# Stated VectorE order and chunk-innermost scan states in an S5/gMLP encoder layer

## The chip, the cores and the metric

The kernel runs on one core of a Trainium2 chip. The metric is the device time of one execution in microseconds (us). The engines are TensorE (PE in the profile; PEld is its weight load), VectorE (DVE), ScalarE (ACT), GpSimd (POOL) and SyncE (SP, which only issues DMAs).

## The reference, cut to what matters

One encoder layer over 512 tokens of width 1024, in float32. The change touches the S5 branch and whatever shares VectorE with it.

```python
n = rms_norm(h, mix_norm_g[i])
proj = n @ w_in[i]                      # xa | zu | zv | gate_a | gate_b
ya = s5_branch(xa, ...)                 # two directions of a diagonal recurrence, 32 groups of 16 channels, 64 states each
yb = sgu_branch(zu, zv, ...)            # gelu, layer norm, 128x128 position mixing per head
merged = gate_a * (ya @ w_proj_a[i]) + gate_b * (yb @ w_proj_b[i])
h = h + merged @ w_out[i]
h = h + memory_cross_attention(...)
h = h + swiglu(...)
return rms_norm(h, final_norm_g)
```

In the S5 branch a state follows `s[t] = lam_bar * s[t-1] + b_bar u[t]` in complex numbers, forward for the first direction and backward for the second, and the output is `Re(c s) + d u`.

## The kernel before, in words

**Weights.** Each float32 product is made of three products of a high and a low half. A weight block (512 KB, 128x1024) is loaded to a `raw` tile, ScalarE casts the high half `whi` (L85) and VectorE subtracts to get the low half `wlo` (L86), both in `split`. `next_w(i)` (L322) hands out block i and traces the split of block i+2 and the load of block i+3. There are three places each for raw, hi and lo, so a split needs the block three before it to be used up. A full block is 24 matmuls of 128x512 (L350).

**The order of the main work.** `tokm` makes the first half of the gate input V (four blocks; the last two are held until all four token tiles have used both), two `feat` pairs make xa (four blocks), `tokm` makes the second half of V (four), then come gate a (eight blocks, "ga"), the eight head products `psv` (L1092, each evacuated by VectorE at L1093), zu (eight blocks, with VectorE work for two heads at L1106 and L86 after every second block), and then gate b and projection b in turn (sixteen). The layer norm of the gate (`layer_norm`, L1019) is a chain VectorE, ScalarE, VectorE, GpSimd, ScalarE, traced once for each token tile during the first ga blocks.

**S5 beside it.** S5 is a Python generator, `s5_program` (L955), which `tick` (L442) advances after each main block. A tick of a full block adds 5.2 x RATE = 5.2 x 0.8 = 4.16 us of credit, and each yield spends what it names: 1.1 for an operation of `s5_input` or `s5_kernels`, 0.8 for a step of the scan. `later(n, fn)` traces `fn` n blocks later. So the place of each S5 instruction in the traced (stated) order is fixed by the ticks. The order on each engine's queue is then made by the scheduler, which may let a ready instruction pass a waiting one; `in_order` (L93) ties one instruction behind the one traced just before it on its engine.

The parts of S5: `s5_setup` (L607, a chain of some 60 small operations), `s5_input(n)` for eight input sets (three VectorE operations of 128x1024 each, then `turn`, eight transposes), `s5_kernels(o)` for four octets of groups (six VectorE operations, then `products`, `store`, `spill` to DRAM and `load` back), `apply` (L880: eight products of an input set with u), `keep` (L888: ScalarE copies the result from PSUM to the states `zh`), `s5_scan` (L893: 62 steps over the 64 chunks, four dependent VectorE operations of 128x64 each), and `s5_outputs(o)` (L904: ScalarE copies the shifted states to `ss`, `mix_` multiplies, `squash`, `back` and `emit` finish).

`zh` is laid out as partition, chunk, part, group: a step of the scan reads and writes 64 neighbouring numbers, and `keep` and the `ss` copies turn the layout with strides of 64 numbers. The two directions sit on partitions 0 to 63 and 64 to 127.

Of the kernel before, what the change touches and what calls it, by code (L numbers as in the profile page):

```python
# [9 lines left out]
F32 = mybir.dt.float32  # L10
# [7 lines left out]
P = 128  # L18
# [34 lines left out]
def hybrid_layer_kernel(  # L53
# [378 lines left out]
    def later(n, fn):  # L432

        side["later"].append((side["now"] + n, fn))
# [93 lines left out]
    def slot(tag, shape, dt, name):  # L528
        return sp.tile(list(shape), dt, tag=tag, name=name)
# [239 lines left out]
    def s5_kernels(o):  # L769

        gs = slice(o * GO, (o + 1) * GO)
        cr, ci = st["c"]
        pr, pi = st["pe"]
        es = []
        for i in range(2):
            e = s5p.tile([P, GO, Q, C], F32, tag="e%d" % i, name="e%d" % i, bufs=2)
            w = s5p.tile([P, GO, Q, C], F32, tag="etmp", name="etmp")
            V.tensor_tensor(e, outer(cr, gs, Q), inner((pr, pi)[i], gs, C), ALU.mult)
            yield 1.1
            V.tensor_tensor(w, outer(ci, gs, Q), inner((pi, pr)[i], gs, C), ALU.mult)  # L780
            yield 1.1
            if i == 0:
                V.tensor_tensor(e, e, w, ALU.subtract)
            else:
                V.scalar_tensor_tensor(glc(e), glc(e), -1.0, glc(w), ALU.mult, ALU.subtract)
            es.append(e)
            yield 1.1
        def products():
            bd = []
            for i in range(2):  # L790
                t = s5p.tile([P, GO, 2, C], F32, tag="bd", name="bd", bufs=2)
                nc.gpsimd.memset(t, 0.0)
                for d in range(2):
                    hf = slice(64 * d, 64 * d + 64)
                    nc.scalar.copy(t[hf, :, d, :], st["b"][i][hf, gs, :])
                bd.append(t)
            ps = aux("pk", (P, 2, P))
            for q in range(2):
                for i in range(2):
                    for j in range(4):  # L800
                        g = 4 * q + j
                        in_order(nc.tensor.matmul(ps[32 * j:32 * j + 32, q, :],
                                                  bd[i][:, g].rearrange("p d c -> p (d c)"), lc(es[i], g),
                                                  start=(i == q == 0), stop=False, tile_position=(0, 32 * j),
                                                  skip_group_check=True))
                for i in range(2):
                    for j in range(4):
                        g = 4 * q + j
                        in_order(nc.tensor.matmul(ps[32 * j:32 * j + C, q, 0:C], bd[i][:, g, 1, :],
                                                  es[i][:, g, Q - 1, :], start=False, stop=(i == 1),  # L810
                                                  tile_position=(0, 32 * j), skip_group_check=True))
            later(0.5, lambda: store(ps))

        def store(ps):
            ks = s5p.tile([P, 2, P], F32, tag="y", name="ks")
            dd = s5p.tile([P, 2, C], F32, tag="dd", name="dd", bufs=2)
            in_order(V.tensor_tensor(dd, st["dmask"].unsqueeze(1).to_broadcast([P, 2, C]),
                                     st["dcol"][:, 2 * o:2 * o + 2].unsqueeze(2).to_broadcast([P, 2, C]), ALU.mult))
            nc.scalar.copy(ks, ps)
            V.tensor_tensor(ks[:, :, 0:C], ks[:, :, 0:C], dd, ALU.add)  # L820
            later(1, lambda: spill(ks))

        def spill(ks):
            kd = dp.tile([GO, C, 15, C], F32, name=f"kd{o}")
            for j in range(4):
                kdj = kd.rearrange("(q j) c l e -> j c q (l e)", j=4)[j]
                nc.gpsimd.dma_start(kdj[:, :, 7 * C:15 * C], ks[32 * j:32 * j + C])
                nc.gpsimd.dma_start(kdj[:, :, 0:7 * C], ks[32 * j + C:32 * j + 2 * C, :, 0:7 * C])
            later(2, lambda: load(kd))

        def load(kd):
            tt = s5p.tile([P, GO, P], F32, tag="tt", name="tt", bufs=2)
            kf = kd.rearrange("g c l e -> c g (l e)")
            for l in range(Q):
                nc.gpsimd.dma_start(tt[l::Q], kf[:, :, (7 - l) * C:(15 - l) * C])
            st["oct", o] = (es[0], es[1], tt)

        later(1, products)
        yield 0.1

# [3 lines left out]
    def s5_input(n):  # L844

        o, i = SETS[n]
        gs = slice(o * GO, (o + 1) * GO)
        br, bi = st["b"]
        pr, pi = st["pw"]
        wt = (wsx[:, 2], wsx[:, 3], inx[:, 0], inx[:, 1], inx[:, 2], inx[:, 3])[n % 6]  # L850
        while n >= 6 and len(applied) < n - 5:
            yield None
        e = wt.rearrange("p g (c l) -> p g c l", c=C)
        w = s5p.tile([P, GO, C, Q], F32, tag="etmp", name="etmp2")
        V.tensor_tensor(e, inner(br, gs, Q), outer((pr, pi)[i], gs, C), ALU.mult)
        yield 1.1
        V.tensor_tensor(w, inner(bi, gs, Q), outer((pi, pr)[i], gs, C), ALU.mult)
        yield 1.1
        V.tensor_tensor(e, e, w, (ALU.subtract, ALU.add)[i])
        later(0.5, lambda: turn(n, wt))  # L860
        yield 1.1
# [8 lines left out]
        later(0.5, lambda: ready.append((n, wt)))  # L870

    def pump():
        if "u" in st and ready:
            n, wt = ready.pop(0)
            apply(*SETS[n], wt)
            applied.append(n)
        if len(applied) < len(SETS):
            later(0.5, pump)

    def apply(o, i, wt):  # L880
        zh = st["zh"]
        ps = aux("pz", (P, GO, NCH))
        for g in range(GO):
            nc.tensor.matmul(ps[:, g, :], wt[:, g, :], st["u"][:, o * GO + g, :], start=True, stop=True)  # L884
        zv = zh[:, :, i, o * GO:(o + 1) * GO].rearrange("p n g -> p g n")
        later(0.5, lambda: keep(zv, ps))

    def keep(zv, ps):  # L888
        nc.scalar.copy(zv[lo_], ps[lo_])
        nc.scalar.copy(zv[hi_], ps[hi_, :, ::-1])  # L890
        st["nz"] = st.get("nz", 0) + 1

    def s5_scan():  # L893
        zh = st["zh"]
        for n in range(1, NCH - 1):
            a = s5p.tile([P, 2, G], F32, tag="sa", name="sa", bufs=2)
            b = s5p.tile([P, 2, G], F32, tag="sb", name="sb", bufs=2)
            V.tensor_tensor(a, zh[:, n - 1], st["ca"], ALU.mult)
            V.tensor_tensor(b, zh[:, n - 1, ::-1, :], st["cb"], ALU.mult)
            V.tensor_tensor(a, a, zh[:, n], ALU.add)  # L900
            V.tensor_tensor(zh[:, n], a, b, ALU.add)
            yield 0.8

    def s5_outputs(o):  # L904
# [3 lines left out]
        e_re, e_im, tt = st["oct", o]  # L908
        zh, u = st["zh"], st["u"]
        ss = s5p.tile([P, 2, GO, NCH], F32, tag="wt", name="ss", bufs=2)  # L910
        ss = (ss[:, 0], ss[:, 1])
        for i, s in enumerate(ss):
            zv = zh[:, :, i, gs].rearrange("p n g -> p g n")
            nc.gpsimd.memset(s[lo_, :, 0:1], 0.0)
            nc.gpsimd.memset(s[hi_, :, NCH - 1:NCH], 0.0)
            nc.scalar.copy(s[lo_, :, 1:NCH], zv[lo_, :, 0:NCH - 1])  # L916
            nc.scalar.copy(s[hi_, :, 0:NCH - 1], zv[hi_, :, 0:NCH - 1][:, :, ::-1])

        yt = tt.rearrange("p (i r) c -> p i r c", i=2)

# [12 lines left out]
        def squash(ps):  # L933

            nc.scalar.activation(yt[:, 0], ps, AF.Gelu_apprx_tanh)
            later(0.5, back)

        def back():
            ps = aux("pyt", (P, GO // 2, P))
# [14 lines left out]

    def s5_program():  # L955
        yield from s5_setup()
        st["zh"] = s5p.tile([P, NCH, 2, G], F32, name="zh")
        later(0.5, pump)
        for n in range(6):
            yield from s5_input(n)  # L960
        yield from s5_kernels(0)
        for n in range(6, len(SETS)):
            yield from s5_input(n)
        yield from s5_kernels(1)
        while st.get("nz", 0) < 2 * NO:
            yield None
        yield None
        yield from s5_scan()
        for _ in range(2):
            yield None  # L970
        for o in range(NO):
            yield from s5_outputs(o)
            if o + 2 < NO:
                yield from s5_kernels(o + 2)
# [10 lines left out]
                    side["gen"] = None  # L985


    zt = slot("D", (P, NT, GW), F32, "zt")
    zsum = cp.tile([P, NT, 2], F32, name="zsum")

# [130 lines left out]
    for c0 in range(0, D, 256):  # L1121
        feat(w_in, OFF_GB + c0, xn, KD, gb_evac)
        feat(w_proj_b, c0, yb, KD, pb_evac)
    finish_side()
    s5.close()
    mgx = ExitStack()
    mgp = mgx.enter_context(tc.tile_pool(name="merge", bufs=1))
# [608 lines left out]
```

## Time and profile before

| | |
|---|---|
| median of 3 runs | 886.7 us (886.3 to 888.8) |
| the profiled execution, its own time | 885.71 us |
| its span from first to last instruction | 883.9 us |
| PE busy | 867.2 us (98%) |
| VectorE busy | 623.7 us (71%) |
| ScalarE busy | 477.8 us (54%) |

How to read it: the page gives busy shares; the chain of waits follows the work that ended last back from the end; the groups by line give the mean duration of each kind of instruction; the windows give busy time by stretch. "f32 x62 | 13.9, 224 | 5.7" at the end of a group is: 62 instructions, 13.9 us busy, 224 ns each, 5.7 us of idle time on that engine before them, followed by what ended it. A matmul's end is modelled, so the distance between starts tells its cost better than its duration.

### The profile page before, as it was taken

Reading aid. Unit: us, or ns where it says so; the run is one execution under the profiler, and the core shown is the slowest. Engines: PE = TensorE matmul, PEld = TensorE weight load, DVE = VectorE, ACT = ScalarE, POOL = GpSimd, SP = SyncE. Lnnn points to the kernel's source line nnn. Section 1 sums busy time; section 2 is a strip of 40 time slices with the busy share of each in tenths; the row PEclk is TensorE's granted clock in tenths of the full one; section 3 lists DMA queues with packets and bytes.
Section 4 is the critical chain, followed back from the end, with each engine's and each line's share of the span. In section 5 each row is a group of like instructions: output and inputs, shape, how many; then the busy total and the mean of one; then the engine's idle time right before and its main releaser. Section 6 shows DMA issues by size and latency. Waiting matters only on the chain.

```text
span 883.9 us, 14489 instructions
## 1 busy us (share of the span) xinstructions
PE 867.2 (98%) x5625; PEld 765.1 (87%) x5625; DVE 623.7 (71%) x1020; ACT 477.8 (54%) x702; POOL 99.6 (11%) x162
## 2 busy tenths in 40 slices
PE   9999999999989999999999999999999999999996
PEld 6788888888768888889899878999999999888875
DVE  5699718997542367659757746767877768899875
ACT  6644887245754343548556535545445555556663
POOL 1001045100063010110000001101110110000000
PEclk9999999999999999999999999999999999999999
DMA  9449368975278777925678235536799963256672
GB/s 267 140 108 260 86 167 221 252 183 142 64 182 230 197 237 195 289 84 166 204 226 253 72 102 157 147 101 174 193 216 211 232 164 95 72 168 202 191 246 87
DMA packets 112134, 154.33 MB, mean 175 GB/s; under 512 B 13545, under 2 KB 78593, under 8 KB 112002
## 3 DMA queue, kind: packets, MB, share of 16 engines
q1 hardware_dynamic: 93042, 128.27, 45.8%
q0 software_dynamic: 16432, 24.09, 16.9%
q10 hardware_dynamic: 2592, 1.05, 0.5%
q8 instruction: 44, 0.72, 0.3%
q14 instruction: 24, 0.20, 0.1%
HBM read 146.60 MB, written 38.24 MB: 209 GB/s over the span
## 4 chain that ended last, share of the span: by engine, by line
PE 86%; ACT 5%; DVE 4%; DMA 3%; issue 2%; SPq 1%; POOLq 0%; POOL 0%; ACTq 0%; DVEq 0%
PE pf L350 24%; PE pt L350 16%; PE px L1331 12%; PE dx L350 7%; PE pq L1331 6%; PE dq L350 3%; PE pv L1331 3%; PE qx L1331 2%; PE dv L350 2%; PE po L350 1%; PE qq L1331 1%; DMA xt<-in_x_dram 1%; PE ptr L511 1%; PE pz L884 1%; ACT ss L916 1%
## 5 line engine op out<-in xcount | busy, mean ns | idle before, releaser
L86 DVE TENSOR_TENSOR wlo<-wraw,whi 128x1024 fp32r<-128x1024 f32 (+1 forms) x139 | 165.0, 1187 | 103.3 <-ACT whi L85 98.0
L85 ACT CAST whi<-wraw 128x1024 fp32r<-128x1024 f32 (+1 forms) x139 | 142.3, 1024 | 157.0 <-PE pf L350 43.0
L350 PE MATMUL pf<-xn,whi 128*128 128x512 f32 x448 | 139.9, 392 | 0.0
L350 PEld LDWEIGHTS pf<-xn,whi 128*128 128x128 f32 x448 | 83.5, 188 | 17.4 <-issue 0.5
L350 PE MATMUL pf<-xn,wlo 128*128 128x512 f32 x224 | 87.6, 391 | 0.0
L1331 PE MATMUL px<-fn,whi 128*128 128x256 f32 x480 | 83.3, 276 | 0.0
L1331 PEld LDWEIGHTS px<-fn,whi 128*128 128x128 f32 x480 | 72.4, 188 | 0.3 <-ACT u L1591 0.2
L85 ACT CAST whi<-b 128x1024 fp32r<-128x1024 f32 x40 | 42.1, 1054 | 50.3 <-PE px L1331 27.1
L86 DVE TENSOR_TENSOR wlo<-b,whi 128x1024 fp32r<-128x1024 f32 x40 | 48.9, 1223 | 27.1 <-ACT whi L85 27.1
L1331 PE MATMUL px<-fn,wlo 128*128 128x256 f32 x240 | 66.4, 277 | 0.0
L350 PE MATMUL dx<-whi,s 128*128 128x512 f32 x170 | 53.9, 392 | 1.4 <-ACT whi L85 1.0
L1331 PE MATMUL pq<-s,whi 128*128 128x256 f32 x320 | 55.1, 276 | 0.0
L85 ACT CAST whi<-t 128x1024 fp32r<-128x1024 f32 x30 | 31.6, 1054 | 36.1 <-PE pv L1331 12.9
L86 DVE TENSOR_TENSOR wlo<-t,whi 128x1024 fp32r<-128x1024 f32 x30 | 36.7, 1225 | 19.9 <-ACT whi L85 19.9
L350 PEld LDWEIGHTS pf<-xn,wlo 128*128 128x128 f32 x224 | 42.1, 188 | 8.9 <-issue 0.2
L1331 PEld LDWEIGHTS pq<-s,whi 128*128 128x128 f32 x320 | 48.2, 188 | 0.1
L1331 PEld LDWEIGHTS px<-fn,wlo 128*128 128x128 f32 x240 | 45.1, 188 | 0.0
L1331 PE MATMUL pq<-s,wlo 128*128 128x256 f32 x160 | 44.2, 277 | 0.0
L350 PE MATMUL pt<-whi,xn 128*128 128x512 f32 x128 | 42.7, 407 | 0.0
L350 PEld LDWEIGHTS dx<-whi,s 128*128 128x128 f32 x170 | 31.7, 188 | 8.5 <-ACT whi L85 1.2
L350 PE MATMUL dx<-wlo,s 128*128 128x512 f32 x85 | 33.2, 391 | 0.0
L1331 PEld LDWEIGHTS pq<-s,wlo 128*128 128x128 f32 x160 | 30.1, 188 | 0.0
(422 smaller groups left out, 2159.8 us busy)
## 6 DMA issues: line engine op xcount, KB each, us to landing
wraw<-in_w_in_dram SPq DMA_DIRECT2D x36, 512.0 KB, 5.0
dsum<-in_w_down_dram SPq DMA_DIRECT2D x20, 512.0 KB, 6.7
wraw<-dsum SPq DMA_DIRECT2D x20, 512.0 KB, 3.7
b<-in_w_gate_dram SPq DMA_DIRECT2D x15, 512.0 KB, 3.9
b<-in_w_up_dram SPq DMA_DIRECT2D x15, 512.0 KB, 5.4
wraw<-in_w_down_dram SPq DMA_DIRECT2D x15, 512.0 KB, 3.9
dsum<-in_w_down_dram POOLq DMA_DIRECT2D x10, 512.0 KB, 7.3
dsum<-dsum POOLq DMA_DIRECT2D x10, 512.0 KB, 7.2
```

The source lines that it names most:

```text
L85: hi = nc.scalar.copy(dst_hi, src)
L86: lo = nc.vector.tensor_tensor(dst_lo, src, dst_hi.bitcast(F32), ALU.subtract)
L350: nc.tensor.matmul(ps, a[x], b[y], start=start and i == 0, stop=stop and i == 2, skip_group_check=free)
L511: tr = nc.tensor.transpose(ps[:, j, :], src[:, k * P:(k + 1) * P], ident)
L884: nc.tensor.matmul(ps[:, g, :], wt[:, g, :], st["u"][:, o * GO + g, :], start=True, stop=True)
L916: nc.scalar.copy(s[lo_, :, 1:NCH], zv[lo_, :, 0:NCH - 1])
L1331: nc.tensor.matmul(ps[:, j, :], a[x], b[y], start=start and j == k == i == 0, stop=k == 3 and i == 2, skip_group_check=True)
```

## The change

1. From just before the first main `tokm` to the end of S5, VectorE's instructions are issued in the order in which they are traced (`manual_schedule` for that engine).
2. `zh` becomes partition, part, group, chunk. `keep` is then one copy of 128x512 where it was two of 64x512, and `ss` is made by two copies of 64x1008 where it was four of 64x504. The scan's operations now take every 64th number.
3. `apply` makes two products per group, one for each half of the columns (a strip of 64 each); the second strip is fed u with its chunks reversed. They are tied to the traced order on PE.
4. Input sets 6 and 7 get tiles of the tags e0 and e1 (two places each, shared with `s5_kernels`) instead of reusing the places of sets 0 and 1, and no longer wait for them; `pump` applies up to two sets at a time.
5. The `bd` tiles are made at the start of `s5_kernels`, and four `later` distances change.

```diff
@@ s5_kernels
-        es = []
+        es, bd = [], []
+        for i in range(2):
+            t = s5p.tile([P, GO, 2, C], F32, tag="bd", name="bd", bufs=2)
+            nc.gpsimd.memset(t, 0.0)
+            for d in range(2):
+                hf = slice(64 * d, 64 * d + 64)
+                nc.scalar.copy(t[hf, :, d, :], st["b"][i][hf, gs, :])
+            bd.append(t)
...
-            later(1, lambda: spill(ks))
+            later(0.5, lambda: spill(ks))
...
-            later(2, lambda: load(kd))
+            later(1, lambda: load(kd))
@@ s5_input
-        wt = (wsx[:, 2], wsx[:, 3], inx[:, 0], inx[:, 1], inx[:, 2], inx[:, 3])[n % 6]
-        while n >= 6 and len(applied) < n - 5:
-            yield None
+        wt = (wsx[:, 2], wsx[:, 3], inx[:, 0], inx[:, 1], inx[:, 2], inx[:, 3])[n] if n < 6 else \
+            s5p.tile([P, GO, P], F32, tag="e%d" % i, name="ex%d" % i, bufs=2)
@@ pump, apply, keep
-        if "u" in st and ready:
-            n, wt = ready.pop(0)
-            apply(*SETS[n], wt)
-            applied.append(n)
+        for _ in range(2):
+            if "u" in st and ready:
+                n, wt = ready.pop(0)
+                apply(*SETS[n], wt)
+                applied.append(n)
...
-            nc.tensor.matmul(ps[:, g, :], wt[:, g, :], st["u"][:, o * GO + g, :], start=True, stop=True)
-        zv = zh[:, :, i, o * GO:(o + 1) * GO].rearrange("p n g -> p g n")
-        later(0.5, lambda: keep(zv, ps))
-
-    def keep(zv, ps):
-        nc.scalar.copy(zv[lo_], ps[lo_])
-        nc.scalar.copy(zv[hi_], ps[hi_, :, ::-1])
+            ug = st["u"][:, o * GO + g, :]
+            for j, x in enumerate((ug, ug[:, ::-1])):
+                hf = slice(64 * j, 64 * j + 64)
+                in_order(nc.tensor.matmul(ps[hf, g, :], wt[:, g, hf], x, start=g == 0, stop=True,
+                                          tile_position=(0, 64 * j), skip_group_check=True))
+        later(0.5, lambda: keep(o, i, ps))
+
+    def keep(o, i, ps):
+        nc.scalar.copy(st["zh"][:, i, o * GO:(o + 1) * GO, :], ps)
@@ s5_scan
-            V.tensor_tensor(a, zh[:, n - 1], st["ca"], ALU.mult)
-            V.tensor_tensor(b, zh[:, n - 1, ::-1, :], st["cb"], ALU.mult)
-            V.tensor_tensor(a, a, zh[:, n], ALU.add)
-            V.tensor_tensor(zh[:, n], a, b, ALU.add)
+            V.tensor_tensor(a, zh[:, :, :, n - 1], st["ca"], ALU.mult)
+            V.tensor_tensor(b, zh[:, ::-1, :, n - 1], st["cb"], ALU.mult)
+            V.tensor_tensor(a, a, zh[:, :, :, n], ALU.add)
+            V.tensor_tensor(zh[:, :, :, n], a, b, ALU.add)
@@ s5_outputs
+        nc.gpsimd.memset(ss[lo_, :, :, 0:1], 0.0)
+        nc.gpsimd.memset(ss[hi_, :, :, NCH - 1:NCH], 0.0)
+        nc.scalar.copy(ss[lo_, :, :, 1:NCH], zh[lo_, :, gs, 0:NCH - 1])
+        nc.scalar.copy(ss[hi_, :, :, 0:NCH - 1], zh[hi_, :, gs, 0:NCH - 1][:, :, :, ::-1])
         ss = (ss[:, 0], ss[:, 1])
-        for i, s in enumerate(ss):
-            zv = zh[:, :, i, gs].rearrange("p n g -> p g n")
-            nc.gpsimd.memset(s[lo_, :, 0:1], 0.0)
-            nc.gpsimd.memset(s[hi_, :, NCH - 1:NCH], 0.0)
-            nc.scalar.copy(s[lo_, :, 1:NCH], zv[lo_, :, 0:NCH - 1])
-            nc.scalar.copy(s[hi_, :, 0:NCH - 1], zv[hi_, :, 0:NCH - 1][:, :, ::-1])
...
-            later(0.5, back)
+            later(1, back)
@@ s5_program
-        st["zh"] = s5p.tile([P, NCH, 2, G], F32, name="zh")
+        st["zh"] = s5p.tile([P, 2, G, NCH], F32, name="zh")
@@ before the main work, and after finish_side()
+    ordered = ExitStack()
+    ordered.enter_context(tc.manual_schedule(engines={mybir.EngineType.DVE}))
...
+    ordered.close()
```

More of the change, by code (lines that the diff above doesn't have):

```diff
@@ L788, in products @@
         def products():
[L789 to L796, printed above, removed]
             ps = aux("pk", (P, 2, P))
@@ L880, in apply @@
     def apply(o, i, wt):
-        zh = st["zh"]
         ps = aux("pz", (P, GO, NCH))
         for g in range(GO):
-            nc.tensor.matmul(ps[:, g, :], wt[:, g, :], st["u"][:, o * GO + g, :], start=True, stop=True)
-        zv = zh[:, :, i, o * GO:(o + 1) * GO].rearrange("p n g -> p g n")
-        later(0.5, lambda: keep(zv, ps))
-    def keep(zv, ps):
-        nc.scalar.copy(zv[lo_], ps[lo_])
-        nc.scalar.copy(zv[hi_], ps[hi_, :, ::-1])
+            ug = st["u"][:, o * GO + g, :]
[6 more added lines that the diff above has]
+        nc.scalar.copy(st["zh"][:, i, o * GO:(o + 1) * GO, :], ps)
         st["nz"] = st.get("nz", 0) + 1
```

## The prediction

> **What bounds the kernel now.** I read the page first, then the chain of waits, then the windows around the change, then the groups by line of each kind of instruction.
>
> ```profile
> span 883.9 us, 14489 instructions
> PE 867.2 (98%) x5625; PEld 765.1 (87%) x5625; DVE 623.7 (71%) x1020; ACT 477.8 (54%) x702; POOL 99.6 (11%) x162
> 164.44 48.99 PE pf L350 x216
> 165.00:214.00 49.00, 49.00 (x219) 40.25 (x218) 44.42 (x165) 19.70 (x26) 4.66 (x4) 1.00 0.79 186
> 245.00:294.00 49.00, 46.36 (x336) 37.61 (x335) 14.40 (x17) 23.47 (x30) 22.08 (x42) 1.00 0.81 202
> L898 DVE TENSOR_TENSOR sa<-zh,ca x62: 215/224/228, 130.6 to 216.0; 128x64 f32<-128x64 f32 x62
> ```
>
> TensorE sets the time: it is busy for 98% of the span. In the chain, 216 matmuls take 48.99 us, 0.2268 us each, so a block of 24 is 5.44 us; that is the pace that VectorE must keep. In the same stretch, the second window, VectorE is busy for 44.42 of 49.00 us (the third pair of numbers is DVE): it is nearly full there, and PE still doesn't stop. The last row shows why that works: the 62 scan steps are spread from 130.6 to 216.0 us, 1.4 us per step, behind the splits that PE needs. The scan is the filler. Once VectorE must follow the stated order, it is no filler any more.
>
> **Where the stated order puts the scan.** A full tick gives 4.16 us of credit, so 5 or 6 scan steps, or 3 to 4 operations of 1.1. Following the ticks through the changed code, the last set is kept at the first ga block, and the scan's steps stand at 6, 5, 5, 5, 6, 5 and 5 in the ticks of ga blocks 2 to 8, 7 among the eight head products, and 5, 6, 5 and 2 in the first four zu blocks: 62, all ahead of the second pair's zu evacuation. They are ahead of the splits that follow them, and nothing behind can pass.
>
> **Part 1: VectorE against PE, from the end of V (call it E) to the end of the fourth zu block.** These rows price VectorE's list:
>
> ```profile
> 51.78 2.35 DVE L778 TENSOR_TENSOR e<-raw_c,pe 128x1024 f32<-128x1024 f32 x2
> L85 ACT CAST whi<-wraw 128x1024 fp32r<-128x1024 f32 x50 | 52.5, 1051 | 77.7 <-PE pf L350 42.5 <-DVE sa L898 12.4 <-DMA yd<-tt 9.2
> L1025 ACT ACTIVATE zt<-zt,nm 128x1024 f32<-128x1024 f32 x4 | 4.6, 1149 | 0.6 <-DVE nm L1023 0.5
> L472 ACT ACTIVATE sq<-zt 128x512 f32<-128x512 f32 x8 | 5.0, 626 | 1.4 <-DMA gad<-gas 1.4
> L472 ACT ACTIVATION_READ_ACCUMULATOR sq<-zt 128x1 f32 x8 | 1.5, 187 | 0.0
> L1066 DVE TENSOR_SCALAR mix<-mix,gbc 128x128 f32<-128x128 f32 x8 | 1.8, 294 | 0.0
> L1093 DVE SCALAR_TENSOR_TENSOR sv<-psv,gbc,mix 128x512 f32<-128x512 f32 x8 | 5.8, 744 | 0.0
> L1106 DVE TENSOR_TENSOR zu<-zu,sv 128x512 f32<-128x512 f32 x8 | 5.5, 688 | 2.1 <-ACT zu L1105 2.1
> L86 DVE TENSOR_TENSOR yb_lo<-zu,yb_hi 128x512 fp32r<-128x512 f32 x8 | 5.5, 692 | 0.2
> L85 ACT CAST yb_hi<-zu 128x512 fp32r<-128x512 f32 x8 | 5.0, 622 | 9.7 <-DVE zu L1106 9.7
> 151.40 0.23 DVE L898 TENSOR_TENSOR sa<-zh,ca 128x64 f32<-128x64 f32 x1
> 152.19 0.22 DVE L898 TENSOR_TENSOR sa<-zh,ca 128x64 f32<-128x64 f32 x1
> ```
>
> - V holds its third and fourth block to its end, so the split traced at its fourth block waits for E, and all of VectorE's work behind it too: 1.05 us for the cast.
> - 14 splits, from that of the second ga block to that of the seventh zu block, which stands right behind the second pair's evacuation. Each 1.17 us (two neighbours of that size take 2.35): 16.4.
> - two operations of input set 7, six of octet 1 and the row sums, 128x1024 each: 9 x 1.17 = 10.5.
> - four layer norms. VectorE's two halves of each are traced together, so VectorE stands still between them while ScalarE does L1025 and two sums of squares: 1.15 + 2 x (0.63 + 0.19) = 2.8, with the small operations 3.1; four make 12.4. Queued behind that wait are the next split and the scan.
> - mixing 1.8; head evacuations 5.8.
> - zu for four heads: 0.69 + 0.62 (the cast in between) + 0.69 = 2.0 each: 8.0.
>
> Without the scan that is 55.9. A step now takes 0.79 us (151.40 to 152.19). The new layout makes each of its four operations take one operand with a stride. No row has that on 64 numbers; the nearest have it on 32:
>
> ```profile
> L681 DVE TENSOR_TENSOR pows<-slab 128x32 f32<-128x32 f32 x1 | 0.2, 224 | 0.3 <-ACT slab L669 0.3
> L671 DVE TENSOR_TENSOR slab<-slab 128x32 f32<-128x32 f32 x1 | 0.2, 192 | 0.0
> L723 DVE TENSOR_TENSOR slab<-pows,slab 128x32 f32<-128x32 f32 x1 | 0.2, 207 | 0.0
> L722 DVE TENSOR_TENSOR slab<-slab 128x32 f32<-128x32 f32 x1 | 0.2, 185 | 0.0
> ```
>
> L681 writes every ninth number, L671 neighbours: 32 ns more, 1.0 ns a number. L723 reads every ninth number, L722 neighbours: 22 ns more, 0.7 a number. For 64 numbers, three reads and one write: 3 x 44 + 64 = 196 ns, so a step of 0.986 us; 62 make 61.1. The bounds are 0 (0.79, 49.0) and 64 ns for all four (1.046, 64.9); I take the rows by kind. The Trainium skill's page "SBUF — State Buffer" (The DMA port swizzle) says that an access stays at full speed only while consecutive ones hit the same 16-byte line, and each crossing pays; it speaks against this layout, reads and writes alike. By that rule alone the four would pay alike, the sum 3.8 us higher; the trace agrees on the write, and shows the read cheaper (22 against 32 ns).
>
> VectorE is thus through with its list at E + 55.9 + 61.1 = E + 117. PE, unhindered, needs that last split after 14 blocks (76.2), the head products and a few pieces of S5:
>
> ```profile
> 162.39 2.05 PE psv L1092 x16
> 98.25 3.52 PE pz L884 x32
> 72.41 0.87 PE pw L868 x8
> ```
>
> Head products: 64 at 2.05 / 16 = 8.2. S5's own after E: one turn 0.9, two applies 3.5, one octet's products, about 1.4 (an estimate between turn and apply): 5.8. So PE is there at E + 90. **PE stalls for 117 - 90 = 27 us**, in pieces before the splits and, at the head products, on PSUM banks that wait for L1093 behind scan steps. Bounds: without the stride price and with half of the layer norms' wait hidden, 27 - 12 - 6 = 9; with 64 ns on all and each of the layer norms' ScalarE work behind one more cast (4 x 1.05), 35.
>
> **Part 2: the beginning.** In stated order the split of V's fourth block stands behind setup's chain up to the powers.
>
> ```profile
> 35.85 1.23 DVE L86 TENSOR_TENSOR wlo<-wraw,whi 128x1024 fp32r<-128x1024 f32 x1 [2.26 <-ACT whi L85]
> 37.39 0.22 DVE L681 TENSOR_TENSOR pows<-slab 128x32 f32<-128x32 f32 x1 [0.32 <-ACT slab L669]
> L690 DVE TENSOR_TENSOR pows<-pows 128x128 f32<-128x128 f32 x1 | 0.3, 307 | 0.0
> ```
>
> Now it ends at 37.1. The chain gets its sine at 37.39, then has some 22 operations of 0.22 to 0.31 us, which overlap by a third: about 3.6; with the split, 42.2. PE has V's third block for all tokens meanwhile: I take 4 (0 to 5). During xa each tick carries 3.8 operations and a split, 4.8 x 1.17 = 5.6 against 5.44, and it starts late, since the split at V's end waits as at E: 1.6 (0 to 3).
>
> **Part 3: PE's own.** `apply` goes from 128 records of 0.110 (the pz row) to 256 of half the width. The nearest form is the outputs' pair of 64-wide strips:
>
> ```profile
> 258.35 9.30 PE pf L350 x40
> 267.65 2.77 PE py L929 x48
> ```
>
> That is 0.058 each, 14.8 against 14.1; the 40 matmuls ahead of the strips take 0.2 more than 40 x 0.2268, so changing form eight times costs up to 1.6. I take +1.5 (0 to 14, if strips don't overlap). No row shows PE reading in reverse; I put it at nothing, since the py pitch is set by the strip.
>
> **Part 4: what it saves.**
>
> ```profile
> PE pk L802 <- DVE e L785: 1.6, 1, 1.6
> PE pyt L941 <- ACT tt L935: 1.1, 1, 1.1
> L889 ACT COPY zh<-pz 64x512 f32<-64x512 f32 x8 | 8.5, 1057 | 4.2 <-PE pz L884 4.1
> L869 ACT COPY wsx<-pw 128x512 f32<-128x512 f32 x8 | 4.5, 587 | 3.1 <-PE pw L868 3.1
> L916 ACT COPY ss<-zh 64x504 f32<-64x504 f32 x8 | 8.7, 1092 | 0.1
> ```
>
> Two PE waits, 2.7 us, are the whole idle time of the window 245 to 294 (46.36 of 49.00): the later `back` removes one, octets further ahead the other: -2.7 (0 to -5). The longer distance to `back` takes away the second; the first waits for the kernel operations, with which nothing else competes on VectorE there once the scan is over. ScalarE gets back 8 x (2 x 1.06 - 0.59) + 4 x (4 x 1.09 - 2 x 1.05) = 21 us (the new `ss` copies by the cast's 128x1024). I count that at nothing more on PE: PE's blocks cover those copies now, and if the cover were thinner than it looks, the end of -5 holds it. The `bd` copies move past nothing that waits. Spill and load move forward on POOL's queue; priced as a rival.
>
> **Sum:** 27 + 4 + 1.6 + 1.5 - 2.7 = +31.4 on the profiled 885.7: 917.1. The median of the runs shown is 1.0 above the profiled execution: 918. The ends of the known terms are +5 and about +46.
>
> **Rivals.**
> - *VectorE stays ahead; the saving decides (faster).* It needs VectorE's list at or under E + 90: no stride price (-12), the layer norms' waits gone (-12) and 3 more. For it: PE doesn't stop now with VectorE 91% busy. Against: the steps move from after the splits to before them. It gives 1.5 - 5 = -3.5, 883. Chance 0.08; part way to it, within 0.3%, 0.04.
> - *The stride costs nothing on 64 numbers.* Then Part 1 is 15 and the time 906. For it: strided rows here are few and short. Against: L889 against L869. Chance 0.15.
> - *The pinned `mix_` waits for its kernel.* After the change spill to mix is 2 blocks, 10.9 us, for octets 2 and 3. Eight issues and landings each way need more:
>
> ```profile
> kd<-ks POOLq DMA_DIRECT2D x8, 16.0 KB, 4.5
> tt<-kd POOLq DMA_DIRECT2D x16, 64.0 KB, 5.7
> L835 POOL DMA_DIRECT2D tt<-kd x32 | 17.7, 671 | 6.0 <-DMA dsum<-in_w_down_dram 2.8 <-DMA kd<-ks 2.6 <-issue 0.5
> ```
>
>  An issue is 17.7 / 32 = 0.55. So 8 x 0.55 + 4.5 + 8 x 0.55 + 5.7 = 19, 8 short, twice: 934. It decides only if no later block goes ahead on PE; those blocks aren't tied. Chance 0.10.
> - *Sets 6 and 7 don't get places of their own.* Octet 1 and set 6 share e0's two places, so VectorE may wait for the apply; a block at most: 923. Chance 0.05.
>
> **Numbers.** The forecast has 0.58. Over 0.3% (2.7 us, about what a measurement of this kernel tells from no change): slower 0.58 + 0.15 + 0.10 + 0.05 = 0.88; same 0.04; faster 0.08. The range from 898 to 936 takes in the forecast, the free stride, the late kernel and the shared places, and leaves out the faster cases and the far ends.
>
> **What would show it.** Right: PE waiting for `wlo` L86 and on L1093 in ga, psv and zu, 20 us or more of lost pace between E and the fifth zu block; VectorE over 95% occupied or standing before the layer norm's L1028; scan operations of 260 to 285 ns; a scan some 65 to 80 us long. `keep` copies of 0.59 and `ss` copies of 1.05 us. Wrong: scan operations still at 220 ns, or PE at 5.44 us a block throughout ga and zu, or the loss after 245 us.

## The result and the profile after

| kernel | median, us | range | profiled execution, its span |
|---|---|---|---|
| before | 887.75 | 886.3 to 889.0 (4 runs) | 885.71, 883.9 |
| after | 916.09 | 914.3 to 916.7 (4 runs) | 916.23, 914.5 |

After against before is 1.0317 (95% interval 1.0292 to 1.0341): 28.3 us slower. The prediction was 918.0 us, with a range from 898 to 936.

The page of the changed kernel, engine totals and two rows of its forty slices (each slice is 22.9 us):

```profile
span 914.5 us, 14710 instructions
PE 877.4 (96%) x5753; PEld 768.3 (84%) x5753; DVE 635.0 (69%) x1020; ACT 452.0 (49%) x682; POOL 99.6 (11%) x154
PE   9899997788999999999999999999999999999996
PEclk9999998989899999999999999999999999999999
```

PE is still the busiest engine, but it has holes in slices 1, 2 and 7 to 10. The windows there, and the two that the prediction showed of before (us of the window, then PE, PEld, DVE, ACT and POOL busy; the granted clock is the third number from the end):

```profile
105.00:154.00 49.00, 41.92 (x349) 32.59 (x348) 28.38 (x77) 27.97 (x48) 17.60 (x33) 0.96 0.45 124
154.00:203.00 49.00, 38.43 (x178) 32.78 (x177) 45.02 (x177) 12.23 (x19) 7.50 (x12) 0.87 0.65 170
203.00:232.00 29.00, 25.48 (x105) 19.89 (x104) 21.82 (x65) 13.86 (x18) 3.48 (x3) 0.94 0.58 138
165.00:214.00 49.00, 41.14 (x193) 34.93 (x193) 45.46 (x168) 11.65 (x16) 3.53 (x3) 0.91 0.66 167
245.00:294.00 49.00, 49.00 (x405) 40.06 (x405) 23.70 (x27) 20.29 (x29) 19.64 (x38) 1.00 0.71 177
```

From 165 to 214 us PE had been busy for all 49.00 us beside 44.42 of VectorE. Now VectorE has 45.46 there, and PE only 41.14. In the first window VectorE is busy for 28.38 of 49 us and PE stands all the same: VectorE isn't full there, it waits. In the last one, PE's 2.6 us of idle time are gone. What PE waited for longest, and below it three of VectorE's waits (us in all, times, longest):

```profile
PE psv L1092 <- DVE sv L1093: 7.1, 1, 7.1
PE pf L350 <- DVE wlo L86: 5.6, 4, 2.3
PE pt L350 <- DVE wlo L86: 4.3, 2, 3.6
PE pf L350 <- ACT whi L85: 4.1, 3, 2.2
PE psv L1092 <- ACT gas L1075: 3.4, 3, 2.7
```

```profile
DVE ms L1028 <- ACT sq L472: 13.1, 4, 4.4
DVE yb_lo L86 <- ACT yb_hi L85: 9.8, 8, 4.3
DVE e L785 <- PE pz L885: 6.4, 1, 6.4
```

These are the waits that the prediction named (`wlo` L86, L1093, the layer norm's L1028), and two that its sum did not hold: `e` of octet 1 for the apply of set 6, and a long one at `yb_lo`. PE's waits for `whi` and `gas` are on ScalarE. In its timeline the longest of them, 2.7 at `gas`, is an operation at 162.50 that stood 5.9 us for an earlier `gas` to be stored to DRAM; that one (155.55) came right behind the sums of squares of the last layer norm. The waits of before for `pk` and `pyt` are gone.

### The profile page after: what moved, and what is told of

It is laid out like the page before. It is cut to its first block, busy times and chain, and to the rows that moved or that the text cites. A ratio compares the mean times of both kernels' runs of the same rounds, so it can differ in the third digit from the quotient of the medians.

```text
span 914.5 us, 14710 instructions
## 1 busy us (share of the span) xinstructions
PE 877.4 (96%) x5753; PEld 768.3 (84%) x5753; DVE 635.0 (69%) x1020; ACT 452.0 (49%) x682; POOL 99.6 (11%) x154
## 3 DMA queue, kind: packets, MB, share of 16 engines
q10 hardware_dynamic: 2592, 1.05, 0.4%
## 4 chain that ended last, share of the span: by engine, by line
PE 82%; DVE 10%; ACT 2%; DMA 2%; issue 1%; SPq 0%; POOL 0%; POOLq 0%; DVEq 0%; ACTq 0%
PE pf L350 22%; PE pt L350 16%; PE px L1332 12%; PE dx L350 6%; PE pq L1332 6%; PE dq L350 3%; PE pv L1332 3%; PE qx L1332 2%; DVE wlo L86 2%; PE dv L350 2%; DVE zh L901 2%; DVE sa L898 1%; DMA slab<-in_s_log_step_dram 1%; PE py L927 1%; PE po L350 1%
## 5 line engine op out<-in xcount | busy, mean ns | idle before, releaser
L86 DVE TENSOR_TENSOR wlo<-wraw,whi 128x1024 fp32r<-128x1024 f32 (+1 forms) x139 | 164.9, 1187 | 102.0 <-ACT whi L85 101.7
L350 PE MATMUL pf<-xn,whi 128*128 128x512 f32 x448 | 142.5, 403 | 4.2 <-ACT whi L85 4.1
L350 PEld LDWEIGHTS pf<-xn,whi 128*128 128x128 f32 x448 | 86.0, 194 | 24.4 <-ACT whi L85 5.9
L86 DVE TENSOR_TENSOR wlo<-b,whi 128x1024 fp32r<-128x1024 f32 x40 | 48.9, 1223 | 28.6 <-ACT whi L85 28.6
L86 DVE TENSOR_TENSOR wlo<-t,whi 128x1024 fp32r<-128x1024 f32 x30 | 36.7, 1225 | 19.9 <-ACT whi L85 19.9
L1332 PE MATMUL pq<-s,wlo 128*128 128x256 f32 x160 | 44.3, 277 | 0.0
L350 PE MATMUL pt<-wlo,xn 128*128 128x512 f32 x64 | 26.4, 415 | 4.3 <-DVE wlo L86 4.3
```

What stands on the lines that cost most here:

```text
L86: lo = nc.vector.tensor_tensor(dst_lo, src, dst_hi.bitcast(F32), ALU.subtract)
L350: nc.tensor.matmul(ps, a[x], b[y], start=start and i == 0, stop=stop and i == 2, skip_group_check=free)
L1332: nc.tensor.matmul(ps[:, j, :], a[x], b[y], start=start and j == k == i == 0, stop=k == 3 and i == 2, skip_group_check=True)
```

## The experiments

Two theories stood against each other. **Order:** in stated order VectorE's list becomes the bound from the end of V on, and everything else is small. **Layout:** the strides and strips cost the time, and the order alone would change little. Times of before in the two groups of runs were 888.46 and 887.1 to 887.2 us; ratios are against these.

**Before with the stated order and nothing else.**

```diff
+    ordered = ExitStack()
+    ordered.enter_context(tc.manual_schedule(engines={mybir.EngineType.DVE}))
...
+    ordered.close()
```

> The kernel before with the stated VectorE order alone; layout, strips, places and distances as before. The order theory: the waits that VectorE now stands through (end of V, four layer norms, zu) and the scan ahead of the splits cost 27 - 12 (no stride price) + 4 + 1.6 = about 20 us: 905 to 910. The layout theory (the strided scan is what costs): the order alone is nearly free, 886 to 891.

914.98 us (913.8 to 916.4), 1.03 (1.0282 to 1.0318): +26.5. The order alone makes nearly all of the loss, more than was expected, and the layout theory falls. Its waits on VectorE:

```profile
DVE ms L1030 <- ACT sq L472: 20.8, 4, 7.9
DVE yb_lo L86 <- ACT yb_hi L85: 19.9, 8, 10.2
```

Where ScalarE has the strided copies of the old layout (`keep`, and eight `ss` copies in a row), the same two waits are longer than in the changed kernel.

**The changed kernel without the stated order.**

```diff
-    ordered = ExitStack()
-    ordered.enter_context(tc.manual_schedule(engines={mybir.EngineType.DVE}))
...
-    ordered.close()
```

> The changed kernel without the stated order; everything else as changed. The order theory: splits pass the scan again, the scan's 62 x 0.17 = 10.5 us more of VectorE are mostly hidden, and the strips (256 records at 0.0315 instead of 128 at 0.110) give 6 us back: 878 to 890. The layout theory: most of the loss stays, 905 or more.

877.5 us (876.8 to 878.4), 0.9878 (0.9863 to 0.9893): 11 us faster than before, a little under the range expected, and with one other version the fastest kernel here. The same stretches, in its windows:

```profile
105.00:154.00 49.00, 49.00 (x380) 40.77 (x373) 40.83 (x141) 29.50 (x53) 26.40 (x43) 1.00 0.78 215
154.00:203.00 49.00, 48.05 (x232) 39.93 (x232) 47.42 (x150) 16.23 (x22) 5.86 (x5) 1.00 0.75 195
```

```profile
L898 DVE TENSOR_TENSOR sa<-zh,ca x62: 251/267/275, 114.9 to 210.1; 128x64 f32<-128x64 f32 x62
```

The scan's steps are as dear as in the changed kernel (267 ns, below), VectorE is busy for 47.42 of 49 us, and PE doesn't stop: as a filler, the dear scan costs nothing. The order costs 38.6 us on this version (877.5 to 916.1) and 26.5 on the old one.

**The changed kernel with the old layout of `zh`, order kept.**

```diff
-        st["zh"] = s5p.tile([P, 2, G, NCH], F32, name="zh")
+        st["zh"] = s5p.tile([P, NCH, 2, G], F32, name="zh")
```

(with `keep`, the scan and the `ss` copies indexed to match)

> The changed kernel with the old layout of the states (scan on neighbours, one strided keep copy, four strided ss copies); the order stays. The order theory: only the stride's 62 x 0.17 = 10.5 us come back, less some ScalarE time: 904 to 910. The layout theory: 885 to 892. If the stride is hidden: 914 to 918.

913.23 us (909.7 to 913.8), 1.027 (1.0243 to 1.0297): only 2.9 below the changed kernel, outside the 904 to 910 that the order theory expected. The scan's steps are cheap again, reads and writes, but the eight `ss` copies stand ahead of the second pair's `yb_hi` cast on ScalarE:

```profile
L898 DVE TENSOR_TENSOR sa<-zh,ca x62: 212/224/227, 136.4 to 213.3; 128x64 f32<-128x64 f32 x62
L901 DVE TENSOR_TENSOR zh<-sa,sb x62: 224/225/227, 136.9 to 213.8; 128x64 f32<-128x64 f32 x62
```

```profile
DVE yb_lo L86 <- ACT yb_hi L85: 15.8, 8, 8.8
```

So the new layout takes about 10 us on VectorE, and gives most of it back on ScalarE, behind which VectorE stands: 6.0 of it show at this wait. The wait at `ms` is 13.2 here, as in the changed kernel, so the 20.8 of the order alone doesn't come from the layout by itself.

**Both undone: bd, distances (spill, load and `back`), own places and strips alone.** (the two edits above together)

> The changed kernel with neither the stated order nor the new layout: strips fed in reverse, bd early, own places, the new distances. The order theory: the strips' 6 us and the two PE waits of 2.7 us come out as time, 878 to 884. Rival (the strips' saving is hidden by VectorE or lost in the queue order): 885 to 889.

877.83 us (877.2 to 878.0), 0.988 (0.9865 to 0.9894). The layout makes no difference where VectorE may choose (877.5 with it).

**Order kept, the layer norm's second half traced a block later.**

```diff
             sum_sq(ss[:, i:i + 1], z[:, HALF[i]])
+        later(1, lambda: layer_scale(z, ss, ms, r))
+
+    def layer_scale(z, ss, ms, r):
         nc.vector.tensor_tensor(ms, ss[:, 0:1], ss[:, 1:2], ALU.add)
```

> The changed kernel, order kept, with the second half of each layer norm (the two small VectorE operations, GpSimd, the scaling) traced one block later, so that VectorE no longer stands between the halves. The waits theory: the 13.1 us for which VectorE stood before L1028 come out of its list, and up to that much out of the time: 902 to 907. If VectorE's list is not what sets the time there: 913 or more.

907.03 us (905.5 to 907.8), 1.0224 (1.0207 to 1.0241): -9.1. VectorE's wait for the sums of squares:

```profile
DVE ms L1031 <- ACT sq L472: 3.6, 2, 3.4
```

The wait went from 13.1 to 3.6, 9.5 us less, and the time gained 9.1: a microsecond for a microsecond, as it must be if VectorE's list is the bound there.

**Order kept, the scan paced by 1.2 us of credit a step instead of 0.8.**

```diff
-            yield 0.8
+            yield 1.2
```

> The changed kernel, order kept, with a scan step at 1.2 of credit instead of 0.8, so 3.5 steps in a block instead of 5.2. The place theory (the scan stands ahead of the splits that PE needs): 19 steps of 0.96 fewer ahead of the seventh zu block's split, 18 us back, some 4 us lost again in the later zu blocks: 899 to 907. If the standing waits alone are the cost: 913 or more.

905.61 us (904.3 to 906.9), 1.0205 (1.0186 to 1.0225): -10.5. Fewer steps stand ahead of each split, and the queue on L1093 shrinks from 7.1 to 1.8; but S5 ends later, and PE waits for its result:

```profile
PE pf L350 <- DMA ygt<-yd: 6.3, 1, 6.3
PE psv L1092 <- DVE sv L1093: 1.8, 1, 1.8
```

**Order only from the second half of V on.** (the two lines that begin the order stand just before `tokm(w_in, OFF_V + 512, ...)`)

> The changed kernel with the stated order from the second half of V on only; V's first half and xa in free order. By the terms of Part 2: 4 + 1.6 us back, 909 to 912. If the slower start of the ordered kernels (the first weight matmul at 12.4 instead of 9.6 us) comes from the order too, 3 more: 906 to 909.

910.7 us (909.7 to 914.0), 1.0274 (1.0251 to 1.0297): -5.4, the price of the beginning. In the profiled executions the first half of V ends at 44.8 instead of 50.4 us. This one also had the faster of the two paces of the first matmuls (last section); the strips alone, in free order too, had the slower and ended that half at 44.5, so nothing is taken off for the pace.

**The three together.** (the three edits above)

> The changed kernel with three edits at once that stood alone in other runs: the layer norm's second half traced one block later (there -9.1), 1.2 us of credit for a step of the scan (-10.5), the stated order only from the second half of V on (-5.4). If the stalls lie one behind the other in one list of VectorE, each edit takes away its own and they add: 916.1 - 25 = 891 (888 to 894), a little slower than the kernel before, with waits of PE of 6 us left before the outputs of S5. If they cover each other in part (a step of the scan moved away from one splits' queue lands in the place that the layer norm's wait left), less: 896 to 900. If the order had a cost besides the list, not less than 900.

894.63 us (893.7 to 895.7), 1.0087 (1.0072 to 1.0102): -21.5 of the -25 that the three gave apart. They nearly add. The two longest waits that are left are no longer on VectorE's list:

```profile
PE pf L350 <- ACT yg_hi L85: 5.6, 1, 5.6
PE ptr L511 <- issue: 3.1, 1, 3.1
```

The first is S5's end, late by the slower pacing; the second is in the first 25 us.

**Before with the strips alone (one strided `keep` copy, free order).**

```diff
-            nc.tensor.matmul(ps[:, g, :], wt[:, g, :], st["u"][:, o * GO + g, :], start=True, stop=True)
+            ug = st["u"][:, o * GO + g, :]
+            for j, x in enumerate((ug, ug[:, ::-1])):
...
-        nc.scalar.copy(zv[lo_], ps[lo_])
-        nc.scalar.copy(zv[hi_], ps[hi_, :, ::-1])
+        nc.scalar.copy(zv, ps)
```

> The kernel before with the strips alone: apply as two strips, the second fed in reverse, and keep as one strided copy of 128 partitions; free order, old layout, places and distances. The strips theory: 256 records at 0.0315 (8.1 us) for 128 at 0.110 (14.1): 6 us back, 881 to 884. If the 11 us of the unordered kernels come from the distances and bd: 886 to 889.

883.71 us (880.6 to 889.4, 10 runs), 0.9966 (0.9947 to 0.9985): -3.4. The outputs come earlier, and meet a kernel that isn't back from DRAM:

```profile
PE py L932 <- DMA tt<-kd: 3.3, 1, 3.3
```

With the change's shorter way to the kernel (spill and load sooner) this wait is absent, in the version without the order too. Behind the wait the granted clock is at half for another 3.4 us, from 279.8. The two would explain by their size why strips and shorter distances bring more together than the strips alone; the distances by themselves were not run.

**The version without the order, with one wide product for each group again.**

```diff
-            for j, x in enumerate((ug, ug[:, ::-1])):
...
+            nc.tensor.matmul(ps[:, g, :], wt[:, g, :], st["u"][:, o * GO + g, :], start=True, stop=True)
...
-        nc.scalar.copy(st["zh"][:, i, o * GO:(o + 1) * GO, :], ps)
+        zv = st["zh"][:, i, o * GO:(o + 1) * GO, :]
+        nc.scalar.copy(zv[lo_], ps[lo_])
+        nc.scalar.copy(zv[hi_], ps[hi_, :, ::-1])
```

> The changed kernel without the stated order, and with one wide product for each group in apply instead of two strips (keep is two copies again, the second reversed). It splits the 11 us that the rest of the change saves. If the strips bring it, as the version with strips alone (-3.3) and their pitch (about 6 us of TensorE) say: 877.5 + 3 to 6 = 881 to 884. If the kernels' earlier places (bd, spill, load, back, own places of sets 6 and 7) bring it: 877 to 879.

887.8 us (885.8 to 890.0, 10 runs), 1.0007 (0.9993 to 1.0021): no gain is left, outside both expectations. Undoing the strips takes away 10.3 us. Some 6 of these are PE's own time for them (next section). Another 2.8 show as a wait at the head products, which in the version with strips is 0.9:

```profile
PE psv L1088 <- DVE sv L1089: 3.7, 2, 2.8
```

Why VectorE is late there without the strips was not found; in free order the scheduler places its work anew in each version. Not all of the 10.3 is the strips': in the profiled executions (spans of 887.5 and 875.0 us) this version ends the first half of V 2.0 us later (44.3 against 42.3), before either has run a strip or a product in its place. Its granted clock is 0.50 from 18.1 to 21.3 us, where the other has 1.00.

## Why the prediction was right, by its own steps

**Part 1 (27): the mechanism and nearly the size.** VectorE's rows at the two ends of the list:

```profile
106.65 1.23 DVE L86 TENSOR_TENSOR wlo<-wraw,whi 128x1024 fp32r<-128x1024 f32 x1 [11.78 <-ACT whi L85]
229.90 2.35 DVE L86 TENSOR_TENSOR wlo<-wraw,whi 128x1024 fp32r<-128x1024 f32 x2
```

E is 106.65 less the cast, 105.6; the first of the two splits at 229.90 is the seventh zu block's and ends at 231.1. The list took 125.5 us, 117 predicted. By its terms:
- The scan. Its four operations:

```profile
L898 DVE TENSOR_TENSOR sa<-zh,ca x62: 250/264/275, 136.6 to 221.5; 128x64 f32<-128x64 f32 x62
L899 DVE TENSOR_TENSOR sb<-zh,cb x62: 247/255/265, 136.7 to 221.7; 128x64 f32<-128x64 f32 x62
L900 DVE TENSOR_TENSOR sa<-sa,zh x62: 252/263/275, 136.9 to 221.8; 128x64 f32<-128x64 f32 x62
L901 DVE TENSOR_TENSOR zh<-sa,sb x62: 266/274/282, 137.2 to 222.1; 128x64 f32<-128x64 f32 x62
```

 260 to 285 ns were forecast, and L899 lies just under; the read of L898 costs 40 ns more than with the old layout, the write of L901 49. The distance from step to step is 0.959 us (0.986 predicted), 59.5 for 62. The steps stand in the places that were forecast, but the whole scan lasts 85.8 us (136.6 to 222.4), longer than the 65 to 80 given as a sign.
- The layer norms' waits, 13.1 against 12.4.
- Missed: `e` of octet 1 stood 6.4 us for the apply of set 6 (the fourth rival's mechanism; it was given less than a block and 0.05 as a case of its own, and came as a term beside the others).
- Missed: ScalarE's `ss` copies ahead of `yb_hi`, on which VectorE stood 4.34 us where 0.62 was counted. In ScalarE's timeline:

```profile
222.45 1.04 ACT L913 COPY ss<-zh 64x1008 f32<-64x1008 f32 x1 [1.88 <-DVE zh L901]
225.60 1.03 ACT L914 COPY ss<-zh 64x1008 f32<-64x1008 f32 x1
226.66 0.62 ACT L85 CAST yb_hi<-zu 128x512 fp32r<-128x512 f32 x1
```

Together 6.4 + 3.7 + 0.7 - 1.6 = 9.2 over the forecast, 8.5 measured. Against PE's E + 90 that list gives 35 us. Adding up how far each distance between matmul starts exceeds full pace (0.227 us for 512 columns, 0.110 for 128 or 64) gives 35.1 us from 100 to 240, and 4.9 in the same window of before. So the price was 30.2, not 27: 8.5 us of list were missed, and the 5 that PE already lost there were not taken off.

**Part 2 (4 and 1.6).** The first power and the split behind the chain, in VectorE's timeline:

```profile
38.54 0.21 DVE L681 TENSOR_TENSOR pows<-slab 128x32 f32<-128x32 f32 x1
42.91 1.22 DVE L86 TENSOR_TENSOR wlo<-wraw,whi 128x1024 fp32r<-128x1024 f32 x1
```

The split ended at 44.1, predicted 42.2: the powers began 1.15 us later than in before, and took 4.4 where 3.6 was estimated. The same sum from 20 to 60 us is 7.6 against 2.8: 4.8, and 5.4 by the order begun later. During xa nothing was lost beyond before: the 1.6 is wrong, by its small size.

**Part 3 (+1.5): the wrong sign.** The chain's rows of the strips:

```profile
91.08 2.01 PE pz L885 x64
97.80 3.88 PE pz L885 x128
```

0.031 us each, so 256 take 7.9 where 128 wide ones took 14.1: a gain of 6.2. The prediction priced a strip by the pitch of the `py` row, 0.058, which has 128 moving columns; these have 64. The Trainium skill's page "TensorEngine Tiling (Array Packing)" (Key Properties) says that tiles in different places of the array load weights and multiply in parallel; the trace agrees: a pair takes 0.062 us, a wide product of 64 columns 0.110.

**Part 4 (-2.7).** Both waits are gone; the sum from 240 to 300 fell by 3.1. But "ScalarE's 21 us count at nothing more" was wrong in stated order: the old layout's copies stand ahead of what VectorE waits for, and the run with them gains only 2.9 from its cheaper scan. The 904 to 910 expected of the old layout in stated order fails for that reason: 913.2. The rival of a free stride (906) falls with the scan's rows above. A `ss` copy takes 1.03 to 1.04 us, as forecast (1.05).

**The sum.** 30.2 + 4.8 - 6.2 - 3.1 is 25.7 of the 30.6 by which the span grew. Another 2.6 lie in the first 20 us (last section) and some 2 are not assigned. That 31.4 came so near owes something to errors that cancelled: +8.5 and -5 in Part 1, and about -7.7 in Part 3. The ends of +5 and about +46 don't come out of the terms: with the bounds as stated, Part 3's 14 among them, they add up to +4 and +57.

**Adding what doesn't add.** The rest of the change brings 11 us without the order and nothing with it (914.98 to 916.09). By the same sum of distances the order alone loses some 8 us less from 100 to 240 us than the changed kernel and some 2 more from 240 to 300, and it lacks the 6.2 that the strips save: together nothing. That time which PE saves came back as a longer wait on VectorE's list would fit this; no run separates it from what the scan and `e` add to the list.

**The rivals.** VectorE didn't stay ahead. `mix_` didn't wait for its kernel: PE shows no wait at `py`.

## What to carry to other kernels

Before an engine is made to follow a stated order, list what it executes between two points at which another engine needs it, waits included, and compare that with the other engine's pace; a long dependent chain is a good filler only as long as urgent work may pass it. Every instruction in that order that waits for another engine is charged to all behind it, so trace the second half of a chain over two engines at least one block later. Savings that come together with such an order may not show (here 11 us without it, nothing with it): try them without the order first.

## What the runs showed of the hardware

**A stall slows PE after it.** Granted clock in three windows that begin as a wait ends:

```profile
44.10:47.40 3.30, 3.22 (x8) 2.57 (x9) 3.06 (x19) 1.71 (x3) 0.00 (x0) 0.50 0.48 159
143.00:146.50 3.50, 3.09 (x7) 2.51 (x8) 0.78 (x5) 2.48 (x5) 1.21 (x1) 0.52 0.86 290
187.00:190.00 3.00, 2.87 (x13) 2.90 (x14) 2.93 (x12) 0.00 (x0) 0.00 (x0) 0.50 1.02 155
```

PE's timeline in the second of them:

```profile
144.86 0.63 PE L350 MATMUL pf<-xn,wlo 128*128 128x512 f32 x1
145.28 1.06 PE L350 MATMUL pf<-xn,whi 128*128 128x512 f32 x2
146.14 0.58 PE L350 MATMUL pf<-xn,wlo 128*128 128x512 f32 x1
```

From start to start a matmul of 512 columns takes 0.43 us there (0.86 for the two at 145.28) instead of 0.227. In the first two windows there are seven or eight such, some 1.5 us lost each time; in the third, those of the head products take 0.213 instead of 0.111. They follow waits of 3.6, 1.7 and 2.0 close together, and 7.1 us. Three more stretches begin as waits of 2.3, 2.7 and 2.2 us end. From 20 to 240 us the clock is at half for 27 us in all in the changed kernel (mean granted clock 0.94), and never in before and in the version without the order (1.00). What this costs lies inside the stalls as counted above; how much of it is on the path, where VectorE is late anyway, was not separated. The Trainium skill's page "TensorE: Matmul & The Clock Gate" (HAM oscillation — how this bites in real kernels) tells of idle gaps over about 3.4 us, after which PE runs at half rate; the trace agrees on the half rate, and shows it after shorter gaps too (2.3 us alone; 1.7 and 2.0 close together).

**The first matmuls have two paces.** By groups, of after and then of before:

```profile
L567 PE MATMUL pg<-g_row,ones x4: 1056/1056/1218, 5.6 to 8.3; 1*128 1x512 f32 x4
```

```profile
L567 PE MATMUL pg<-g_row,ones x4: 587/587/692, 5.2 to 6.6; 1*128 1x512 f32 x4
```

The first weight matmul came at 12.40 us in the one and 9.56 in the other. Order alone had 1056, order from the second half of V 587, strips alone without order 1056: it doesn't go with the change. The same page of the Trainium skill (Part 1: The HAM clock gate) says that the gate's window runs freely, so that where the first matmuls fall in it differs from run to run; that fits what the traces record. In each execution the granted clock changes only on a grid of 3.41 us. In the six profiled executions with 587 ns it is first recorded at full, and for 3.41 us only, from 3.9 to 5.8 us after the start; in the six with 1056 the first such record is at 13.3 to 13.9. So the pace goes with where the grid falls at the start, in one execution of each kernel.

**Strided operands of 64 numbers on VectorE** cost 40 ns (read) and 49 ns (write) over neighbours, 0.6 and 0.8 ns a number, a little below the rows of 32 on which the forecast stood (0.7 and 1.0). The Trainium skill's page "SBUF — State Buffer" (Door 1: The DMA port swizzle) has each access that crosses to a new line pay, and doesn't tell reads from writes; the trace agrees that both pay, and the write is again the dearer.
